# A hybrid DeltaNet and HGRN2 block on one core: gate weights loaded a block ahead, sums of x a pair ahead, and part of a branch's products moved into the first gate's pass

## The chip, the cores and the metric

The kernel runs on one core of a Trainium2 chip. A core has TensorE (PE, the matrix engine), VectorE (DVE), ScalarE (ACT), GpSimd (POOL) and SyncE (SP); here every transfer between DRAM and the on-chip memory is issued from SP's one queue, which is worked off in order. The metric is the device time of one execution in microseconds. Three runs of the kernel before gave 1931.05 us as their median (1929.38 to 1932.9).

## The reference

One layer over 2048 tokens of width 1024, with 16 meta tokens in front. One projection of the normalized input feeds two branches and two gates; the branches are projected back, gated, added and projected out:

```python
proj = rmsnorm(h, norm_w) @ w_in
a_q, a_k, a_v, a_beta, a_alpha, a_z, b_q, b_f, b_i, b_g, gate_a, gate_b = split(proj)
y_a = rmsnorm(gated_deltanet(conv(a_q, a_k, a_v), a_beta, a_alpha), gnorm_a) * silu(a_z)
y_b = rmsnorm(hgrn2(b_q, b_f, b_i), gnorm_b) * silu(b_g)
mixed = sigmoid(gate_a) * (y_a @ w_branch_a) + sigmoid(gate_b) * (y_b @ w_branch_b)
out = rmsnorm(h + mixed @ w_out, final_norm_w)[:, N_META:]
```

The two gates are products of 2048 x 1024 by 1024 x 1024 each, and so is the last projection; w_branch_a and w_branch_b are 512 x 1024.

## The kernel before

**Numbers.** Everything is float32. A large matmul is done with each operand split into two float16 parts (high, and the residual low), as three products of parts. To prepare a weight means: load it raw, take statistics (ACT squares with a sum, or DVE a largest value), find one power of two as its scale, multiply by it (DVE, L212 and L214), round to the high part (ACT, L215), and subtract that for the residual (L216, on DVE or GpSimd). `prepare` is a generator, and one step of it is a block of the statistics or one of eight k-blocks of the split.

**Work units.** Tokens go in 17 chunks of 128 (chunk 0 holds the meta tokens) and, where two go together, in eight pairs. Five stages follow one another:

1. To about 576 us: norm of x, pair by pair (stored as `xs_d`), the projections of the HGRN2 branch b and its chunked scan. `levels` (L684) alternates DVE products QK (L682) with PE matmuls `pl` (L705, L710). As a background, each chunk also runs 2 steps of a weight preparation for branch a's k and v, and 3 steps of the gate weights.
2. 576 to 720 us: the transition, with convolutions of branch a's first pairs and its q and z weights.
3. 720 to about 1290 us: the DeltaNet branch a (convolutions, an inverse by recursion, the scan `scan2`); beside its last pair the first gate's products of pairs 0 and 1.
4. To about 1440 us: the first gate's pass, pairs 2 to 7, with 9 background steps a pair that prepare w_branch_a, w_branch_b and the two halves of w_out.
5. To the end: for each pair the second gate's products, then `merge` for each of its chunks: branch a (24 matmuls `pbr` on w_bra and two additions to the first gate's value), branch b (24 on w_brb), the mix, its split and transposes (`mT`), the 48 matmuls of the last projection (`pout`), the final norm and the store.

**The gates by seven products.** A gate's product for a pair is done as a Strassen-Winograd scheme: a 2 x 2 block product with seven products P1 to P7 for eight, done in the order P1, P2, P6, P7, P5, P3, P4, each of 12 matmuls (`gate_pair`, L446): 84 matmuls a pair. P1, P2 and P4 take x itself, the other four take `xs`, four sums of blocks of x. `left` (L410) makes the sums: seven additions and subtractions on DVE (L428 to L436), three on GpSimd (L439 to L441), and for each sum its high half on ACT (L422) and its low half on DVE (L423); they are kept in `ss_d` for the second gate. `add` (L466) adds each product to its outputs on DVE, and `end` (L469) takes the tanh; the first gate's values go to `ga_d`.

**The gate weights.** `gate_steps` (L343) loads a gate's raw weight in four blocks twice: once for the statistics (even blocks by ACT, L367, odd ones by DVE, L360), once for the seven factors (L377 scales, L381 rounds, L383 and L385 subtract, L392 to L399 form differences). Raw blocks go through one buffer, `gx`; finished factors through three buffers `go` to DRAM (`wg_d`). `gate_part` (L403) reads them back two products at a time, 2 MB. The second gate's first part is requested ahead of the first gate's pass, its other three behind it.

**What sets the order.** Instructions are put in a list per engine by a scheduler that simulates a timeline; `tc.high_priority` draws an instruction ahead, and `tc.issue_after` holds one back. The order on each engine is then fixed, and each engine waits in order. A buffer of a pool is written again only when its last reader is done.

Of the kernel before, what the change touches and what calls it, by code (L numbers as in the profile page):

```python
# [34 lines left out]
POOLC = (3,)  # L35
LAST = (8, 12)
# [23 lines left out]
def hybrid_kernel(ctx: ExitStack, tc: tile.TileContext, x, meta_tokens, norm_w, w_in, conv_w, a_log,  # L60
# [17 lines left out]
    gx = ctx.enter_context(tc.tile_pool(name="gx", bufs=1))  # L78
# [124 lines left out]
    def split_steps(begun, dve=(), scale=None):  # L203
# [16 lines left out]
    def prepare(begun, dst, dve=((), ())):  # L220

        wsl[dst] = yield from split_steps((yield from stats_steps(begun, dve[0])), dve[1],
                                             V)
# [119 lines left out]
    def gate_steps(i, off, pool):  # L343
# [3 lines left out]
        src = w_in[0][:, off:off + D].rearrange("(a k p) (b n) -> p k a b n", a=2, p=P, b=2)  # L347
        stats = tp.tile([P, 16], F32, tag="stats16", name="stats16", bufs=1)
        rows = nw.rearrange("p (a k) -> p a k", a=2)

        def load(k):
            t = gx.tile([P, 2, 2, 512], F32, tag="t8", name="graw")
            for a in range(2):
                SY.dma_start(t[:, a], src[:, k, a])
            return t
        for k in range(4):
            t = load(k)
            st = stats[:, 4 * k:4 * k + 4]
            if k % 2:
                V.tensor_reduce(st, t.rearrange("p a b n -> p (a b) n"), AX.X, ALU.max, apply_absolute_value=True)  # L360
                for a in range(2):
                    V.tensor_scalar(st[:, 2 * a:2 * a + 2], st[:, 2 * a:2 * a + 2], rows[:, a, k:k + 1], None, ALU.mult)
                V.tensor_tensor(st, st, st, ALU.mult)
            else:
                for j in range(4):
                    junk = sp.tile([P, 512], F16, tag="junk", name="junk", bufs=1)
                    A.activation(junk, t[:, j // 2, j % 2], AF.Square, scale=rows[:, j // 2, k:k + 1],  # L367
                                 accum_out=st[:, j:j + 1])
            yield
        sc = scale_of(stats, 16, f"g{i}", GEXP)  # L370
        V.tensor_scalar(hu[:, i:i + 1], sc[:, 1:2], 0.5, None, ALU.mult)
        fac = tp.tile([P, 2, 4], F32, tag="gfac", name="gfac", bufs=1)
        V.tensor_scalar(fac, rows, sc[:, 0:1], None, ALU.mult)
        for k in range(4):
            t = load(k)
            for a in range(2):
                A.activation(t[:, a], t[:, a], AF.Copy, scale=fac[:, a, k:k + 1])  # L377

            def put(n, b, f):
                o = pool.tile([P, 2, 512], F16, tag="go", name="go", bufs=3)  # L380
                A.activation(o[:, 0], b, AF.Copy, scale=f)  # L381
                if f == 1.0:
                    V.tensor_tensor(o[:, 1], b, o[:, 0], ALU.subtract)  # L383
                else:
                    V.scalar_tensor_tensor(o[:, 1], b, f, o[:, 0], ALU.mult, ALU.subtract)  # L385
                SY.dma_start(wg_d[i][:, ORDER.index(n), k], o)
            b11, b12, b21, b22 = t[:, 0, 0], t[:, 0, 1], t[:, 1, 0], t[:, 1, 1]
            put("P1", b11, 1.0)
# [965 lines left out]
```

## Time and profile before

| what | value |
|---|---|
| median of three runs | 1931.05 us (1929.38 to 1932.9) |
| the profiled execution | 1930.47 us, its span 1928.7 us |
| mean granted clock of PE | 0.95 |
| busy in the span: PE, DVE, ACT, POOL | 1747.4, 1360.7, 932.3, 305.2 us |
| instructions | 42,889 |
| moved by DMA | 184.73 MB, mean 96 GB/s |

A busy time is the sum of an engine's instructions, a share is of the span. The granted clock is PE's, as a part of the full speed of 2.4 GHz; a mean below 1 is a mixture with the lower level of 1.2 GHz, at which a matmul of the same shape takes longer. A gap in a row is the idle time of that engine just before the instruction, with the instruction that ended it. The rows themselves stand in a section of their own below.

### The profile page before, as it was taken

How to read it: one execution, taken by the hardware profiler on the slowest of the kernel's cores; microseconds unless marked ns; L12 is line 12 of the kernel's file. 1: busy time of each engine (PE TensorE's matmuls, PEld its weight loads, DVE VectorE, ACT ScalarE, POOL GpSimd, SP SyncE). 2: the span in 40 equal slices, each digit the busy share in tenths (PEclk: the TensorE clock that was granted, in tenths of full speed). 3: DMA queues.
4: the chain of work that ended last, by engine and by line, in shares of the span. 5: the costliest groups of instructions: out<-in, count | busy, mean ns of one | idle time of the engine just before them, and what ended most of it. 6: DMA issues, size and time to landing. Idle time of an engine off the chain costs nothing. (4 is left out here: it accounts for less than half of the span.)

```text
span 1928.7 us, 42889 instructions
## 1 busy us (share of the span) xinstructions
PE 1747.4 (91%) x16763; PEld 1178.6 (61%) x16763; DVE 1360.7 (71%) x5340; ACT 932.3 (48%) x2264; POOL 305.2 (16%) x425
## 2 busy tenths in 40 slices
PE   4599898969999689999999999987789999999997
PEld 3476675746767678888888886553334444444444
DVE  7944776767867978898888799787653444544555
ACT  7655775666756644666656555744321111111211
POOL 3200011101211521222213113233110000000000
PEclk9699899979998889999999999988889999999999
DMA  9013323234250010100100032634373322332121
GB/s 351 33 57 104 123 92 127 100 110 149 78 176 30 12 51 23 40 13 7 34 30 7 13 116 78 229 128 168 143 293 126 121 79 97 101 123 80 58 82 50
DMA packets 56399, 184.73 MB, mean 96 GB/s; under 512 B 6460, under 2 KB 6644, under 8 KB 49028
## 3 DMA queue, kind: packets, MB, share of 16 engines
q1 hardware_dynamic: 56196, 182.00, 26.7%
q8 instruction: 131, 2.15, 0.5%
q14 instruction: 72, 0.59, 0.1%
HBM read 125.35 MB, written 56.62 MB: 94 GB/s over the span
## 5 line engine op out<-in xcount | busy, mean ns | idle before, releaser
L459 PE MATMUL pgate<-wg,xs 128*128 128x512 f16 x768 | 186.3, 397 | 32.5 <-ACT xs L422 29.7
L259 PEld LDWEIGHTS <-x 128*128 128x128 f16 x1368 | 131.7, 99 | 94.9 <-issue 3.3
L1279 PE MATMUL pout<-w_o,mt 128*128 128x512 f16 (+1 forms) x792 | 170.9, 373 | 1.7 <-ACT mt L1267 0.9
L459 PEld LDWEIGHTS <-xs 128*128 128x128 f16 x768 | 77.0, 102 | 127.5 <-ACT xs L422 31.7
L318 DVE SCALAR_TENSOR_TENSOR pair<-raw,cw,pair 128x256 f32<-128x256 f32 (+1 forms) x297 | 138.2, 496 | 6.1 <-ACT pair L312 5.7
L459 PE MATMUL pgate<-wg,x 128*128 128x512 f16 x576 | 132.5, 382 | 4.4 <-ACT gt L472 2.9
L1279 PEld LDWEIGHTS <-mt 128*128 128x128 f16 x792 | 76.8, 98 | 89.5 <-DVE mt L1269 2.3
L939 PEld LDWEIGHTS <-y 128*128 128x128 f16 x768 | 74.6, 98 | 87.1
L459 PEld LDWEIGHTS <-x 128*128 128x128 f16 x576 | 56.6, 99 | 71.4 <-issue 6.7
L1281 DVE SCALAR_TENSOR_TENSOR hres<-pout,mm,hres 128x512 f32<-128x512 f32 (+1 forms) x33 | 24.2, 735 | 102.4 <-PE pout L1279 102.4
L259 PE MATMUL pi<-w_bi,x 128*128 128x512 f16 x408 | 93.9, 384 | 0.0
L267 PE MATMUL pq<-x,w_bq 128*128 128x256 f16 x768 | 93.0, 283 | 0.0
L259 PE MATMUL pg<-w_bg,x 128*128 128x512 f16 x384 | 89.3, 382 | 0.0
L939 PE MATMUL pbr<-w_bra,y 128*128 128x512 f16 x384 | 88.6, 379 | 0.0
L939 PE MATMUL pbr<-w_brb,y 128*128 128x512 f16 x384 | 88.1, 379 | 0.0
L267 PEld LDWEIGHTS <-w_ak 128*128 128x128 f16 x864 | 77.6, 99 | 14.2 <-issue 2.4
L267 PEld LDWEIGHTS <-w_aq 128*128 128x128 f16 x864 | 76.6, 99 | 15.7 <-POOL w_aq L216 3.3
L267 PEld LDWEIGHTS <-w_bq 128*128 128x128 f16 x768 | 77.8, 102 | 11.1
L267 PEld LDWEIGHTS <-w_av 128*128 128x128 f16 x864 | 76.1, 99 | 11.0 <-issue 0.7
L267 PE MATMUL pq<-x,w_bf 128*128 128x256 f16 x672 | 80.1, 277 | 0.0
L1032 DVE TENSOR_TENSOR R<-R,U 128x2 f32<-128x2 f32 (+14 forms) x510 | 78.3, 186 | 0.2
L682 DVE TENSOR_TENSOR QK<-QK,Tb 128x1024 f32<-128x1024 f32 x48 | 61.4, 1279 | 23.4 <-PE pl L710 23.4
(475 smaller groups left out, 4010.4 us busy)
## 6 DMA issues: line engine op xcount, KB each, us to landing
x<-xs_d SPq DMA_DIRECT2D x22, 1024.0 KB, 5.9
graw<-in_w_in_dram SPq DMA_DIRECT2D x32, 512.0 KB, 5.0
wg_d<-go SPq DMA_DIRECT2D x56, 256.0 KB, 2.2
wg<-wg_d SPq DMA_DIRECT2D x6, 2048.0 KB, 7.8
hx<-in_x_dram SPq DMA_DIRECT2D x16, 512.0 KB, 4.1
xs_d<-x SPq DMA_DIRECT2D x8, 1024.0 KB, 4.1
ss_d<-xs SPq DMA_DIRECT2D x8, 1024.0 KB, 3.9
ga_d<-gt SPq DMA_DIRECT2D x16, 512.0 KB, 5.9
```

What stands on the lines that cost most here:

```text
L259: T.matmul(po[:, j:j + cols], xt[:, k, xa, c0:c0 + P], wt[:, k, wa, j:j + cols], start=(n == 0), stop=(n == 23))
L267: T.matmul(po, wt[:, k, wa, h * P:(h + 1) * P], xt[:, k, xa, c0:c0 + ncol], start=(n == 0), stop=(n == 23))
L318: V.scalar_tensor_tensor(av, rows(h, j), wv(j), av, ALU.mult, ALU.add)
L459: T.matmul(po, L[n](k, xa), w[ORDER.index(n)][:, k, wa], start=m == 0, stop=m == 11)
L682: V.tensor_tensor(qk, qk, dv, ALU.mult)
L939: T.matmul(pb, y[:, h, xa, :], w[0][:, 4 * i + h, wa, :], start=(n == 0), stop=(n == 11))
L1032: V.tensor_tensor(R[:, e, c:], R[:, e, c:], U[:, e, c:c + 1].broadcast_to([P, n // 2, 16 - c]), ALU.mult)
L1279: T.matmul(po, mt[:, xa, k, :], wo[i][0][:, k, wa, js], start=(n == 0), stop=(n == 23))
L1281: V.scalar_tensor_tensor(h[:, i, js], po, mm[:, 2 + i:3 + i], h[:, i, js], ALU.mult, ALU.add)
```

## The change

- Gate weights. One generator serves both gates. Raw blocks go in turn into the two halves of `gstage`, a slot of the pool for large weights, and the block after next is requested as soon as one has been read; `go` has seven buffers for three; the pool `gx` goes, and the second gate's last part gets a pool `g8`. Each chunk runs 4 steps for 3. v's weights of branch a are requested behind pair 5, in `gstage`'s slot, and are prepared with 4 steps a chunk from pair 6 on.
- Sums of x. `left` for the next pair is issued ahead of the products of this one, in both gates, and its three GpSimd operations go to DVE.
- Weights of the first gate's pass. The multiplication by the scale is done by ACT, all eight residual subtractions by DVE (before, half by GpSimd). 14 steps run behind pair 2, then 8 behind each.
- Branch a. For chunks 7 to 16 its 24 matmuls a chunk and two additions are done in the first gate's pass (`first_branch`, behind the gate of the next pair); the gate's values wait for them in four buffers `tbs`, and their sum goes to `ga_d`. `merge` does branch a for chunks 1 to 6 only.
- All four parts of the second gate's weights are requested behind the first gate's pass.

The diff, cut to its core:

```diff
@@ split_steps and prepare
         w, raw, rows, tag, stats = begun
         with tc.high_priority(offset=OFS):
             sc = scale_of(stats, KT, tag)
+        if scale is A and rows is not None:
+            fac = tp.tile([P, KT], F32, tag="fac", name="fac")
+            V.tensor_scalar(fac, rows, sc[:, 0:1], None, ALU.mult)
         for k in range(KT):
             t = sp.tile([P, 512], F32, tag="st", name="wsc")
-            if rows is not None:
+            if scale is A:
+                A.activation(t, raw[:, k, :], AF.Copy, scale=sc[:, 0:1] if rows is None else fac[:, k:k + 1])
+            elif rows is not None:
                 E.tensor_scalar(t, raw[:, k, :], rows[:, k:k + 1], sc[:, 0:1], ALU.mult, ALU.mult)
             else:
...
+    def gate_steps(offs, stage, pool):
+        raws = stage.rearrange("p k a n -> p (k a n)").bitcast(F32).rearrange("p (s a b n) -> p s a b n", s=2, a=2, b=2)
+        todo = [(i, k) for i in range(2) for _ in range(2) for k in range(4)]
+        at = [0]
+
+        def load():
+            if at[0] < len(todo):
+                i, k = todo[at[0]]
+                src = w_in[0][:, offs[i]:offs[i] + D].rearrange("(a k p) (b n) -> p k a b n", a=2, p=P, b=2)
                 for a in range(2):
+                    SY.dma_start(raws[:, at[0] % 2, a], src[:, k, a])
+            at[0] += 1
+        load()
+        load()
+        yield
+        for i in range(2):
+            for k in range(4):
+                t = raws[:, k % 2]
...
+                load()
+                yield
...
+            for k in range(4):
+                yield from factor_steps(i, k, raws[:, k % 2], fac, pool)
+                load()
...
-                o = pool.tile([P, 2, 512], F16, tag="go", name="go", bufs=3)
+            o = pool.tile([P, 2, 512], F16, tag="go", name="go", bufs=7)
@@ left
-        G.tensor_tensor(u, a(0, 0, 0), a(1, 0, 0), ALU.subtract)
-        G.tensor_tensor(t, a(0, 0, 1), a(1, 0, 1), ALU.subtract)
-        G.tensor_tensor(u, u, t, ALU.add)
+        V.tensor_tensor(u, a(0, 0, 0), a(1, 0, 0), ALU.subtract)
+        V.tensor_tensor(t, a(0, 0, 1), a(1, 0, 1), ALU.subtract)
+        V.tensor_tensor(u, u, t, ALU.add)
@@ first_gate
         add(prod("P4"), (c21, c21))
         end(c21)
-    def first_gate(q):
+    def first_gate(q, xS, ring=None):
+        if ring is not None:
+            gate_pair(0, xS, wga, [ring[:, (2 * q + j) % 4] for j in range(2)])
+            return
         t = [raw_t("gt0").rearrange("p h i -> p (h i)")[:, :D], acc_t("gt1")]
         t = [x.rearrange("p (a n) -> p a n", a=2) for x in t]
-        gate_pair(0, left(q, True), wga, t)
+        gate_pair(0, xS, wga, t)
         for j in range(2):
             SY.dma_start(ga_d[2 * q + 1 + j], t[j])
@@ the loop over pairs of the first stage
                         qx = query(xnext)
                 if p > 0:
                     with tc.issue_after(mark["A"].ins), tc.issue_after(mark["V"].ins):
-                        run_steps(bg, LAST[i] if last else 2)
+                        run_steps(bg, LAST[i] if last else 2 if p < NP_ - 2 else 4)
                         if not last:
-                            run_steps(gsteps, 3)
+                            run_steps(gsteps, 4)
             if p == 0:
-                gsteps = chain(gate_steps(0, OFF_GA, p1), gate_steps(1, OFF_GB, p1))
+                stage = wp.tile([P, KT, 2, 512], F16, tag="w", name="gstage")
+                gsteps = gate_steps((OFF_GA, OFF_GB), stage, p1)
+                run_steps(gsteps, 1)
                 beg["k"] = in_begin(OFF_K, "ak")
+                bg = prepare(beg["k"], "k")
+            if p == NP_ - 3:
+                run_steps(gsteps)
                 beg["v"] = in_begin(OFF_V, "av")
-                bg = chain(prepare(beg["k"], "k"), prepare(beg["v"], "v"))
+                bg = chain(bg, prepare(beg["v"], "v"))
         scan1(*prev)
@@ the first gate's pass
+        def first_branch(q):
+            for j in range(2):
+                t = tbs[:, (2 * q + j) % 4]
+                branch(2 * q + 1 + j, ya_d, wsl["bra"], t)
+                SY.dma_start(ga_d[2 * q + 1 + j], t)
         fnw = p1.tile([P, D], F32, name="fnw")
         SY.dma_start(fnw, final_norm_w.rearrange("(o d) -> o d", o=1).broadcast_to([P, D]))
         beg["bra"] = br_begin(w_branch_a, gna, "bra")
         beg["brb"] = br_begin(w_branch_b, gnb, "brb")
         beg["o0"], beg["o1"] = out_begin(0, wx), out_begin(1, wx)
-        wgb = gate_part(1, 0, wp)
-        bg = chain(prepare(beg["bra"], "bra", ((), EVEN)), prepare(beg["brb"], "brb", ((), EVEN)),
-                   prepare(beg["o0"], "o0", (HALF, EVEN)), prepare(beg["o1"], "o1", (HALF, EVEN)))
-        for q in range(2, NP_):
-            first_gate(q)
-            run_steps(bg, 9)
-        run_steps(bg)
-        wgb += [f for j in (1, 2, 3) for f in gate_part(1, j, wp if j < 3 else gx)]
         tbs = wp.tile([P, KT, 2, 512], F16, tag="w", name="tbs")
         tbs = tbs.rearrange("p k a n -> p (k a n)").bitcast(F32).rearrange("p (c a n) -> p c a n", c=4, a=2)
+        ALL = tuple(range(KT))
+        bg = chain(prepare(beg["bra"], "bra", ((), ALL), A), prepare(beg["brb"], "brb", ((), ALL), A),
+                   prepare(beg["o0"], "o0", (HALF, ALL), A), prepare(beg["o1"], "o1", (HALF, ALL), A))
+        xS = left(2, True)
+        for q in range(2, NP_):
+            xn = left(q + 1, True) if q + 1 < NP_ else left(0, False)
+            first_gate(q, xS, tbs if q >= LAG else None)
+            xS = xn
+            run_steps(bg, 14 if q == 2 else 8)
+            if q > LAG:
+                first_branch(q - 1)
+        run_steps(bg)
+        first_branch(NP_ - 1)
+        wgb = [f for j in range(4) for f in gate_part(1, j, wp if j < 3 else g8)]
         wba, wbb, wo = wsl["bra"], wsl["brb"], [wsl["o0"], wsl["o1"]]
         us = p1.tile([P, 4], F32, name="us")
@@ the last stage
-        def second_gate(q):
-            gate_pair(1, left(q, False), wgb, [tbs[:, (2 * q + j) % 4] for j in range(2)])
+        def second_gate(q, xS):
+            gate_pair(1, xS, wgb, [tbs[:, (2 * q + j) % 4] for j in range(2)])
         def merge(c, tb):
             mix = raw_t("mix").rearrange("p h i -> p (h i)")[:, :D].rearrange("p (a n) -> p a n", a=2)
             SY.dma_start(mix, ga_d[c])
-            branch(c, ya_d, wba, mix)
+            if c <= 2 * LAG:
+                branch(c, ya_d, wba, mix)
             h = acc_t("hres").rearrange("p (a n) -> p a n", a=2)
             SY.dma_start(h, xf[(c - 1) * P:c * P, :].rearrange("t (a n) -> t a n", a=2))
             V.scalar_tensor_tensor(hf, hf, r, fnw, ALU.mult, ALU.mult)
             SY.dma_start(of[(c - 1) * P:c * P, :], hf)
-        second_gate(0)
+        second_gate(0, xS)
         for q in range(NP_):
             if q + 1 < NP_:
-                second_gate(q + 1)
+                second_gate(q + 1, left(q + 1, False))
             for j in range(2):
                 merge(2 * q + 1 + j, tbs[:, (2 * q + j) % 4])
```

Where the instructions now stand, at three places. First, DVE at the sums of x for pair 6. Before, they stand behind the scaling of w_out (`wsc<-w_o`) and an addition of pair 5 (`gt`); `s` is the sum, `s1l` its low parts:

```order
L216 TENSOR_TENSOR w_o_18834<-wsc,w_o_18834 128x512
L214 TENSOR_SCALAR wsc<-w_o_18834,sc_o_19503 128x512
L466 TENSOR_TENSOR gt_19543<-gt_19544,pgate 128x512
L214 TENSOR_SCALAR wsc<-w_o_18834,sc_o_19503 128x512
L428 TENSOR_TENSOR s_19548<-x 128x512
L216 TENSOR_TENSOR w_o_18834<-wsc,w_o_18834 128x512
L429 TENSOR_TENSOR s1l<-x 128x512
L430 TENSOR_TENSOR s_19548<-s_19548,s1l 128x512
L423 SCALAR_TENSOR_TENSOR xs<-s_19548,xs 128x4x128
```

After, for the same pair:

```order
L447 TENSOR_TENSOR s_19457<-s_19457,s1l 128x512
L456 TENSOR_TENSOR s_19472<-x 128x512
L457 TENSOR_TENSOR s3l<-x 128x512
L483 TENSOR_TENSOR tbs<-tbs,pgate 128x512
L440 SCALAR_TENSOR_TENSOR xs<-s_19457,xs 128x4x128
L458 TENSOR_TENSOR s_19472<-s_19472,s3l 128x512
L450 TENSOR_TENSOR s_19457<-s_19457,x 128x512
L966 SCALAR_TENSOR_TENSOR tbs<-tbs,pbr 128x512
L483 TENSOR_TENSOR tbs<-tbs,pgate 128x512
L450 TENSOR_TENSOR s_19457<-s_19457,x 128x512
L440 SCALAR_TENSOR_TENSOR xs<-s_19472,xs 128x4x128
```

The scalings are gone from between them; the additions that stand among them (`tbs<-tbs,pgate`) are those of pair 5, whose products run meanwhile, and one of branch a (`pbr`).

Second, PE at pair 7, from its second product (P2, on x) to the next. Before, P6 on the sums follows at once:

```order
L459 MATMUL pgate<-wg_17638,x 128x512
L459 LDWEIGHTS x
L459 MATMUL pgate<-wg_17638,x 128x512
L459 LDWEIGHTS xs
L459 MATMUL pgate<-wg_17640,xs 128x512
L459 LDWEIGHTS xs
```

After, 13 matmuls of branch a stand in between:

```order
L476 MATMUL pgate<-wg_17623,x 128x512
L476 LDWEIGHTS x
L476 MATMUL pgate<-wg_17623,x 128x512
L964 LDWEIGHTS y
L964 MATMUL pbr<-w_bra,y 128x512
L964 LDWEIGHTS y
L964 MATMUL pbr<-w_bra,y 128x512
```

A wait for the sums of pair 7 would now be met behind these 13 matmuls.

Third, DVE in the first stage at the statistics of the first gate's weights. Before, one reduction of a raw block stands there (the other one is 85 rows behind):

```order
L682 TENSOR_TENSOR QK<-QK,ff 128x2x512
L560 TENSOR_SCALAR Lg<-sg 128x512
L360 TENSOR_REDUCE stats_2452<-graw 128x4
L714 COPY_PREDICATED PD<-k_175,pl 128x64x2
L682 TENSOR_TENSOR QK<-QK,Tb 128x2x256x2
L556 TENSOR_REDUCE ba<-pba 128x8
L631 SCALAR_TENSOR_TENSOR Lg<-sg,Lg 128x512
L362 TENSOR_SCALAR stats_2452<-stats_2452,nw 128x2 x2
L363 TENSOR_TENSOR stats_2452<-stats_2452 128x4
```

After, both odd blocks' reductions stand close together:

```order
L617 SCALAR_TENSOR_TENSOR L<-qx,L 128x512
L372 TENSOR_REDUCE stats_2451<-gstage 128x4
L619 TENSOR_TENSOR qx<-qx,L 128x512
L374 TENSOR_SCALAR stats_2451<-stats_2451,nw 128x2 x2
L708 TENSOR_TENSOR QK<-qx,ff 128x1024
L375 TENSOR_TENSOR stats_2451<-stats_2451 128x4
L372 TENSOR_REDUCE stats_2451<-gstage 128x4
L715 COPY_PREDICATED PD<-k_172,pl 128x256
L702 TENSOR_TENSOR QK<-QK,ff 128x2x512
```

Between the two reductions stand four rows, and the second one reads the half of `gstage` that the first has just freed.

## Rows read from the trace of the kernel before

**Rows 1.** The page's busy time by engine (share of the span, instructions)
```profile
PE 1747.4 (91%) x16763; PEld 1178.6 (61%) x16763; DVE 1360.7 (71%) x5340; ACT 932.3 (48%) x2264; POOL 305.2 (16%) x425
```

**Rows 2.** Busy time by stage: span, PE, PEld, DVE, ACT, POOL, clock, DMA, GB/s
```profile
192.00:576.00 384.00, 336.93 (x4497) 247.32 (x4498) 275.92 (x724) 252.78 (x495) 52.33 (x38) 0.93 0.35 120
576.00:720.00 144.00, 117.53 (x1471) 97.46 (x1469) 115.96 (x415) 87.19 (x245) 48.26 (x61) 0.85 0.09 31
...
1248.00:1440.00 192.00, 153.65 (x819) 74.50 (x818) 139.21 (x372) 77.93 (x162) 50.85 (x40) 0.88 0.49 181
1440.00:1928.70 488.70, 478.23 (x2425) 226.10 (x2423) 236.99 (x486) 83.26 (x135) 0.00 (x0) 0.99 0.28 95
```

**Rows 3.** Timeline of PE, first gate's pass: start, duration, instructions, gap before
```profile
1293.34 5.66 PE L459 MATMUL pgate<-wg,xs 128*128 128x512 f16 x14 [2.19 <-ACT xs L422]
...
1326.01 6.85 PE L459 MATMUL pgate<-wg,xs 128*128 128x512 f16 x24 [6.62 <-ACT xs L422]
...
1353.45 10.52 PE L459 MATMUL pgate<-wg,xs 128*128 128x512 f16 x48
...
1384.87 13.31 PE L459 MATMUL pgate<-wg,xs 128*128 128x512 f16 x48 [12.19 <-ACT xs L422]
...
1415.56 8.14 PE L459 MATMUL pgate<-wg,xs 128*128 128x512 f16 x24 [8.68 <-ACT xs L422]
```

**Rows 4.** Groups by form, 1290 to 1440: busy, mean ns of one, gaps before
```profile
L459 PE MATMUL pgate<-wg,xs 128*128 128x512 f16 x240 | 65.2, 438 | 31.1 <-ACT xs L422 29.7 <-DVE gt L466 1.5
...
L466 DVE TENSOR_TENSOR gt<-gt,pgate 128x512 f32<-128x512 f32 x34 | 22.8, 684 | 39.0 <-PE pgate L459 38.9
L423 DVE SCALAR_TENSOR_TENSOR xs<-s,xs 128x512 f16<-128x512 f32 x19 | 15.6, 834 | 4.2 <-ACT xs L422 3.9
...
L439 POOL TENSOR_TENSOR s<-x 128x512 f32<-128x512 f16 x4 | 6.0, 1500 | 1.5 <-issue 1.3
...
L436 DVE TENSOR_TENSOR s<-s,x 128x512 f32<-128x512 f32 x5 | 3.4, 685 | 0.1
```

**Rows 5.** Timeline of DVE at the sums for pair 6
```profile
1374.88 0.78 DVE L214 TENSOR_SCALAR wsc<-w_o,sc_o 128x512 f32<-128x512 f32 x1
1375.58 0.68 DVE L428 TENSOR_TENSOR s<-x 128x512 f32<-128x512 f16 x1
...
1376.90 1.52 DVE L429 TENSOR_TENSOR s1l<-x 128x512 f32<-128x512 f16 x1
```

**Rows 6.** Timeline of DVE at the second gate's statistics, and its wait, 190 to 576
```profile
387.88 2.29 DVE L360 TENSOR_REDUCE stats<-graw 128x4 f32<-128x2048 f32 x1 [4.33 <-DMA graw<-in_w_in_dram]
...
404.49 2.29 DVE L360 TENSOR_REDUCE stats<-graw 128x4 f32<-128x2048 f32 x1 [2.29 <-DMA graw<-in_w_in_dram]
...
DVE stats L360 <- DMA graw<-in_w_in_dram: 6.6, 2, 4.3
```

**Rows 7.** Timeline of PE at the same place
```profile
391.98 1.06 PE L705 MATMUL pl<-QK 128*32 128x16 f32 x64 [6.72 <-DVE QK L682]
...
410.13 0.61 PE L166 MATMUL np<-stats,k 128*128 128x16 f32 x2 [4.26 <-DVE stats L363]
```

**Rows 8.** Waits of ACT, 190 to 660: total, times, longest
```profile
ACT go L381 <- DMA wg_d<-go: 14.3, 8, 2.7
ACT graw L377 <- DMA graw<-in_w_in_dram: 12.6, 5, 3.5
```

**Rows 9.** Busy time in two stretches of 48 us, columns as in rows 2
```profile
384.00:432.00 48.00, 32.25 (x357) 23.09 (x355) 28.43 (x96) 30.63 (x69) 3.77 (x3) 0.79 0.33 111
...
1152.00:1200.00 48.00, 45.91 (x437) 33.24 (x438) 45.33 (x277) 28.05 (x95) 15.00 (x28) 1.00 0.24 93
```

**Rows 10.** The page's DMA issues: count, KB each, us from issue to landing
```profile
x<-xs_d SPq DMA_DIRECT2D x22, 1024.0 KB, 5.9
graw<-in_w_in_dram SPq DMA_DIRECT2D x32, 512.0 KB, 5.0
...
wg<-wg_d SPq DMA_DIRECT2D x6, 2048.0 KB, 7.8
```

**Rows 11.** Timeline of PE at the second last chunk's end
```profile
1896.79 0.60 PE L1279 MATMUL pout<-w_o,mt 128*128 128x512 f16 x2 [0.73 <-ACT mt L1267]
1897.87 10.10 PE L1279 MATMUL pout<-w_o,mt 128*128 128x512 f16 x46 [0.48 <-DVE mt L1269]
```

More of the change, by code (lines that the diff above doesn't have):

```diff
@@ L35 @@
 POOLC = (3,)
+LAG = 3
 LAST = (8, 12)
@@ L77, in hybrid_kernel @@
     ap = ctx.enter_context(tc.tile_pool(name="ap", bufs=1))
-    gx = ctx.enter_context(tc.tile_pool(name="gx", bufs=1))
     PSUM = {}
@@ L218, in split_steps, with prepare @@
         return w, sc[:, 1:2], sc[:, 0:1]
-    def prepare(begun, dst, dve=((), ())):
-        wsl[dst] = yield from split_steps((yield from stats_steps(begun, dve[0])), dve[1],
-                                             V)
+    def prepare(begun, dst, dve=((), ()), scale=None):
+        wsl[dst] = yield from split_steps((yield from stats_steps(begun, dve[0])), dve[1], scale)
     def run_steps(steps, n=None):
@@ new lines, in gate_steps @@
+        load()
+        load()
+        yield
+        for i in range(2):
+            stats = tp.tile([P, 16], F32, tag="stats16", name="stats16", bufs=1)
+            for k in range(4):
+                t = raws[:, k % 2]
+                st = stats[:, 4 * k:4 * k + 4]
+                if k % 2:
+                    V.tensor_reduce(st, t.rearrange("p a b n -> p (a b) n"), AX.X, ALU.max, apply_absolute_value=True)
+                    for a in range(2):
+                        V.tensor_scalar(st[:, 2 * a:2 * a + 2], st[:, 2 * a:2 * a + 2], rows[:, a, k:k + 1], None, ALU.mult)
+                    V.tensor_tensor(st, st, st, ALU.mult)
+                else:
+                    for j in range(4):
+                        junk = sp.tile([P, 512], F16, tag="junk", name="junk", bufs=1)
+                        A.activation(junk, t[:, j // 2, j % 2], AF.Square, scale=rows[:, j // 2, k:k + 1],
+                                     accum_out=st[:, j:j + 1])
+                load()
+                yield
+            sc = scale_of(stats, 16, f"g{i}", GEXP)
+            V.tensor_scalar(hu[:, i:i + 1], sc[:, 1:2], 0.5, None, ALU.mult)
+            fac = tp.tile([P, 2, 4], F32, tag="gfac", name="gfac", bufs=1)
+            V.tensor_scalar(fac, rows, sc[:, 0:1], None, ALU.mult)
+            for k in range(4):
+                yield from factor_steps(i, k, raws[:, k % 2], fac, pool)
+                load()
@@ new lines, in factor_steps, with put @@
+    def factor_steps(i, k, t, fac, pool):
+        for a in range(2):
+            A.activation(t[:, a], t[:, a], AF.Copy, scale=fac[:, a, k:k + 1])
+        def put(n, b, f):
+            o = pool.tile([P, 2, 512], F16, tag="go", name="go", bufs=7)
+            A.activation(o[:, 0], b, AF.Copy, scale=f)
+            if f == 1.0:
+                V.tensor_tensor(o[:, 1], b, o[:, 0], ALU.subtract)
+            else:
+                V.scalar_tensor_tensor(o[:, 1], b, f, o[:, 0], ALU.mult, ALU.subtract)
+            SY.dma_start(wg_d[i][:, ORDER.index(n), k], o)
+        b11, b12, b21, b22 = t[:, 0, 0], t[:, 0, 1], t[:, 1, 0], t[:, 1, 1]
+        put("P1", b11, 1.0)
+        put("P2", b21, 1.0)
+        put("P3", b22, 2.0)
+        yield
+        V.tensor_tensor(b11, b12, b11, ALU.subtract)
+        put("P5", b11, 2.0)
+        V.tensor_tensor(b12, b22, b12, ALU.subtract)
+        put("P7", b12, 2.0)
+        yield
+        V.tensor_tensor(b22, b22, b11, ALU.subtract)
+        put("P6", b22, 2.0)
+        V.tensor_tensor(b21, b21, b22, ALU.subtract)
+        put("P4", b21, 1.0)
+        yield
@@ L858, in hybrid_kernel @@
                     run_steps(bg)
-                    run_steps(gsteps)
                     xt = xpair(0)
@@ L928, in hybrid_kernel @@
     mp = cg.enter_context(tc.tile_pool(name="mp", bufs=1))
+    g8 = cg.enter_context(tc.tile_pool(name="g8", bufs=1))
     def branch(c, y_d, w, t):
@@ L1202, in hybrid_kernel @@
                         if p == NP_ - 2:
-                            wga = [f for j in range(4) for f in gate_part(0, j, wp if j < 3 else gx)]
+                            wga = [f for j in range(4) for f in gate_part(0, j, wp if j < 3 else g8)]
                 else:
-                    first_gate(i)
+                    first_gate(i, left(i, True))
             xt = xn
```

50 lines of the change are left out of this document (removed).

## The prediction

> **What bounds the kernel now.** I read the share of busy time first [rows 1]: TensorE (PE) works 1747.4 of 1928.7 us, so no more than 181 us of the span are without a matmul, and only where they lie can a reordering win anything. The table by stages [rows 2] says where. In the last stage (from 1440 us) PE is busy for 478 of 489 us at full clock: there is nothing to win there. The two stages to look at are the long first one (192 to 576 us: 47 us without a matmul, granted clock 0.93) and the first gate's pass (1248 to 1440 us: 38 us without a matmul, a mean granted clock of 0.88, that is part of the time at the lower of its two levels, 1.2 instead of 2.4 GHz). The transition between (576 to 720 us) lacks 26 us, but the change barely touches it.
>
> In the first gate's pass the timeline of PE [rows 3] names one waiter: the products on xs, the sums of x. Four waits, 2.19, 6.62, 12.19 and 8.68 us (pairs 3, 4, 6, 7), 29.7 us together, all before the first xs product of a pair, and none for pair 5 (third row), whose sums were early. Other bubbles of the pass (38.35 − 29.7) come to about 8 us. After a long wait the same matmuls run slower: 48 take 10.52 us behind no wait (0.219 us each) and 13.31 us behind the wait of 12.19. Over the window 1290 to 1440 the 240 xs matmuls take 65.2 us [rows 4], against 240 × 0.219 = 52.6 us: 12.6 us are the price of the lower clock level.
>
> Why the sums are late stands in the order of VectorE (DVE), not in the transfer: DVE scales w_o, then begins pair 6's first sum at 1375.58, and its next additions take 1.52 us each [rows 5], where the same form alone takes 0.685 us [rows 4]. The GpSimd sums of the same pair (1.50 us each, rows 4) run beside them.
>
> In the first stage DVE stops at 387.88 for 4.33 us and at 404.49 for 2.29 us, for raw gate weights [rows 6]; PE is out for 6.72 us before 391.98 and 4.26 us before 410.13 [rows 7]. ACT waits 14.3 us for output buffers of the gate weights to be written away and 12.6 us for raw blocks [rows 8]. Around 400 us the clock is 0.79 [rows 9].
>
> **The change, part by part.** All sums are made against the profiled execution, 1930.47 us with a span of 1928.7; the median of the runs is 1931.05, 0.6 us higher.
>
> *The first gate's pass.* In the new order the sums of a pair stand among the additions of the pair before, and 48 matmuls of the first branch stand with each pair from 4 on. PE then has per pair 84 × 0.219 = 18.4 us of gate and 48 × 0.219 = 10.5 us of branch, 28.9 us. DVE has in the same time 10 sums at 0.685 (three of them from GpSimd), 4 splits at 0.83, 7 gate additions and 4 branch additions at 0.684, and at most 8 residuals of weights at about 0.685: 6.9 + 3.3 + 4.8 + 2.7 + 5.5 = 23.2 us. So DVE keeps ahead of PE from pair 4 on, and the scalings of weights, which stood before the sums, have gone to ACT, which is busy for 78 of 192 us there [rows 2]. A load of x lands 5.9 us after its issue [rows 10]; it can start when the pair two before has freed its buffer, so 5.9 us and about 10 us of sums fit into 28.9. Hence the waits of pairs 4, 6 and 7 (27.5 us) go, pair 3's 2.19 us shrinks at best (no branch work yet in its time: 18.4 us of PE against some 20 of DVE). I take 27 of 29.7 us. Of the 12.6 us of slow clock I take 9, since the tail of branch a's scan still makes bubbles of 1 to 2 us near pairs 3 and 4; of the other 8 us, 1. That is −37 us. Bounds: −15 if the fillers and sums only halve the waits and the clock stays; −50 if all waits, all clock and the other bubbles go.
>
> The branch work itself is the same 384 + 384 matmuls, moved by 10 chunks of 24, 53 us, from the last stage, where PE was full: zero in itself. Its transfers go along: per chunk a load of y and a store of the result, both on SP's one queue, which also carries the loads of x. The stores wait for DVE, and the load of the pair after next stands behind two of them. These stores belong to a branch that is done a pair earlier, so I cost this at 0; if it is not, the third rival below has the price.
>
> *A rule that speaks for more.* After each long wait the rows show dearer matmuls. The Trainium skill, "TensorE: Matmul & The Clock Gate", section "HAM oscillation — how this bites in real kernels", says that an idle gap is paid a second time, in a lower clock behind it; by it the whole 12.6 us would come back and the term would be −41 instead of −37. The rows agree in the direction.
>
> *Gate weights in the first stage.* The same 32 steps are done, four a chunk instead of three. With seven output buffers for three the 14.3 us of ACT go; with the raw block requested two blocks ahead most of the 12.6 us go. What PE sees of it: 6.72 and 4.26 us behind statistics, and of ACT's 26.9 us behind factor steps perhaps a quarter, so some 18 us in all, and a little clock. But the statistics are not cured. There are two half-slots, and in the new order the two reductions of a gate stand five rows of DVE apart (below 3 us of work at these row times), while the block between them is asked for only when the first has been read, and takes 5.0 us to land [rows 10]: DVE still waits about 2 to 3 us, now for the first gate too, which had no such wait (only two of DVE's statistics waited in the first stage, rows 6). I take −6: about 10 won in the factor steps, 4 lost or kept in the statistics. Bounds −20 (all waits and the clock of rows 9) and +10 (four new waits of 2.5 us, nothing won).
>
> *v's weights* start about two pairs later; their last 4 steps fall beside the last pair and the convolutions of the transition, where DVE is busy for 116 of 144 us. Four steps are four scalings and residuals; at 0.685 us each that is 4 × 1.37 = 5.5 us, and up to 4 × 2.2 = 9 us where one of the two takes the 1.5 of rows 5; I take about half as hidden beside PE's work: +3 (0 to +8; not below nothing, since the work is the same and only comes where DVE is busier).
>
> *DVE's three more sums* for pairs 0 and 1 fall at 1104 to 1200 us, where DVE is busy for 45.3 of 48 us [rows 9]: 2 × 3 × 0.685 = 4.1 us, most of it where PE has scan work queued: +1 (0 to +4). Here the Trainium skill, "Perfetto Trace Analysis", section "Optimizing Scalar/DVE Operations", speaks against the change: where DVE is saturated, handing work to ScalarE or even GpSimd may pay. By it the term would be the whole +4.1. It adds that the two share a port, and the 1.52 us of rows 5 beside GpSimd agree, so I stay with +1.
>
> *The end.* At the last chunk boundaries PE waits 0.73 + 0.48 us for the transposed mix [rows 11]; with branch a's matmuls gone three such boundaries lack a filler instead of two. +2 (0 to +4).
>
> *Second gate's weights* are all requested after the first pass now; one of four parts was early before. 2 MB land in 7.8 us [rows 10]. Its buffer comes free after the second product of pair 7, with 60 gate matmuls (13 us) and the last branch behind it: 0, hidden by these; 7.8 us if that cover is gone.
>
> Sum: −37 − 6 + 3 + 1 + 2 = −37 us; 1930.5 − 37 = 1893.5, said 1894.
>
> **Rivals.**
> 1. *Only the first pass works, and by half* (waits move to the queue or to pairs 3 and 4, no gain in the first stage): −15 + 6 = −9 to −20, so 1910 to 1922. For it: SP's queue is in order, and the last chunk of the scan still sits in pairs 3 and 4. Against it: 23.2 us of DVE against 28.9 of PE. Chance 0.17.
> 2. *Both stages work fully*: −50 − 20 + 6, about 1867. For it: the chain of cause is the same in rows 3 and 7. Against: the statistics' waits. Chance 0.10.
> 3. *Slower.* One mechanism, on SP: loads of x and of the second gate's weights stand behind stores of branch results that wait for PE. If these stores end late, each pair from 4 to 7 waits for the 5.9 us of its x plus 10 us of sums after it: 16 us each, and the fillers cannot cover it, since they are what the queue waits for. Three such pairs cost 48 us against the 42 (29.7 + 12.6) that are lost now, and 7.8 us come for the weights: +14, about 1944 (1934 if the first stage wins 10, 1960 with a fourth pair). It decides from the point where a store is done later than the end of its pair's last gate product. Chance 0.09.
> 4. *The reordering does nothing*, because the waits that go are replaced one for one: 1930 ± 4. Chance 0.04.
>
> **How the numbers follow.** My forecast (−25 to −50 us) has 0.60, 1894 us, its own range 1881 to 1906. Rival 1 has 0.17, rival 2 0.10, rival 3 0.09, rival 4 0.04. The range for 8 in 10 leaves out most of rivals 3 and 4 and the ends of 1 and 2: 1866 to 1920. 0.2% of the time is 3.9 us, what can be told from no change. Faster 0.87, same 0.04, slower 0.09.
>
> **What would show it.** In the profile after: no wait of PE over 3 us for xs from pair 4 on, 48 xs matmuls of a pair in 10.5 us, the granted clock of the first pass at 0.95 or more; GpSimd with only the scan's last splits there; the stage from the first gate's pass to the end 35 us shorter together. In the first stage: no wait of ACT for stores of gate weights, and PE stops behind a statistics reduction that are shorter, not gone. I am wrong if PE waits for x instead of xs, if SP holds loads of x behind stores of the branch, or if the first stage becomes longer.

## The result, and the profile after

| | before | after |
|---|---|---|
| median of four runs | 1931.97 us (1929.38 to 1933.32) | 1868.49 us (1864.67 to 1870.26) |
| span of the profiled execution | 1928.7 us | 1868.5 us |
| mean granted clock | 0.95 | 0.966 |

The ratio is 0.967 (95% interval 0.9651 to 0.969): 63 us less, where 37 were forecast. The direction held. The time did not keep to the forecast's own range, 1881 to 1906 us: it lies beside the 1867 us of rival 2 (both stages work fully), which had a chance of 0.10. The term of the first gate's pass came out about as forecast; the term of the gate weights was far too small.

The page's busy time by engine, which answers to [rows 1]:

```profile
PE 1734.6 (93%) x16763; PEld 1171.8 (63%) x16763; DVE 1333.9 (71%) x5350; ACT 949.3 (51%) x2296; POOL 251.0 (13%) x385
```

The same number of matmuls takes 12.8 us less of PE's time, at a mean granted clock of 0.966 for 0.95, and the span loses 60.2. To see where, both traces are cut at events that both have: an update of branch b's state by PE (`pu`) near 193 us and the one five pairs later, the first product of branch a's scan (`pks`), the first product of a gate (`pgate`), the end. Before (columns as in rows 2):

```profile
192.50:555.50 363.00, 316.43 (x4314) 231.95 (x4315) 264.34 (x684) 238.03 (x463) 49.91 (x36) 0.92 0.35 120
555.50:762.96 207.46, 180.48 (x2173) 148.43 (x2171) 167.41 (x773) 119.56 (x330) 59.13 (x85) 0.89 0.11 38
762.96:1176.02 413.06, 409.40 (x4563) 352.31 (x4561) 360.78 (x2388) 247.58 (x806) 92.30 (x200) 1.00 0.10 36
1176.02:1928.70 752.68, 697.35 (x3792) 339.99 (x3789) 438.87 (x1169) 205.91 (x424) 68.65 (x69) 0.96 0.35 122
```

After:

```profile
193.20:527.40 334.20, 308.84 (x4313) 226.78 (x4314) 251.54 (x666) 233.71 (x457) 42.66 (x30) 0.96 0.37 128
527.40:739.60 212.20, 181.20 (x2175) 147.42 (x2173) 175.77 (x787) 122.63 (x336) 67.22 (x91) 0.90 0.12 42
739.60:1152.66 413.06, 409.38 (x4562) 352.37 (x4560) 360.66 (x2390) 247.61 (x806) 90.36 (x198) 1.00 0.10 36
1152.66:1868.50 715.84, 688.68 (x3792) 338.24 (x3789) 415.92 (x1177) 224.63 (x456) 15.52 (x30) 0.98 0.36 128
```

Row by row: −28.8, +4.7, 0.0 and −36.8 us (the first mark itself comes 0.7 us later). The first stage's row holds the surprise: PE idles 25.4 us there (334.20 − 308.84) where it idled 46.6, and does the same matmuls in 7.6 us less. What went are waits of PE for VectorE, 37.2 us in the first row before and 15.2 after, most of them of the matmuls `pl` for a QK product. The largest, before and after (total, times, longest; `ba` is a small reduction right behind a QK product):

```profile
PE pl L705 <- DVE QK L682: 11.3, 4, 6.7
PE pl L710 <- DVE QK L682: 10.8, 6, 4.3
```
```profile
PE pl L730 <- DVE ba L576: 7.0, 2, 4.4
PE pl L730 <- DVE QK L702: 4.7, 3, 2.5
```

In the first gate's pass the waits of [rows 3] are gone. The page's groups of the products, for the whole program, before and then after:

```profile
L459 PE MATMUL pgate<-wg,xs 128*128 128x512 f16 x768 | 186.3, 397 | 32.5 <-ACT xs L422 29.7
...
L459 PE MATMUL pgate<-wg,x 128*128 128x512 f16 x576 | 132.5, 382 | 4.4 <-ACT gt L472 2.9
```
```profile
L476 PE MATMUL pgate<-wg,xs 128*128 128x512 f16 x768 | 175.1, 379 | 2.5 <-DVE gt L483 2.5
...
L476 PE MATMUL pgate<-wg,x 128*128 128x512 f16 x576 | 136.4, 388 | 2.0 <-DVE gt L483 2.0
```

30 us of waits and 11.2 us of slow matmuls went with xs. The products on x became 3.9 us dearer, 2.4 of them behind a new wait, in PE's timeline of the changed kernel:

```profile
1332.32 0.60 PE L166 MATMUL np<-stats,k 128*128 128x8 f32 x2 [7.53 <-ACT junk L199]
1332.77 7.77 PE L476 MATMUL pgate<-wg,x 128*128 128x512 f16 x24
1340.37 5.34 PE L476 MATMUL pgate<-wg,xs 128*128 128x512 f16 x24
```

PE stands 7.53 us at the small product that makes w_out's scale, since ACT still takes the statistics of a w_out that was requested only at 1321.4; the next 24 matmuls take 7.77 us for 5.34. (Another 2.0 us lie near 1197, behind four gaps of 0.4 to 1.4 us in branch a's last scan: 12 products on x take 4.75 us there for 2.75.)

In the first stage the waits of DVE for ACT at the gate weights' factors fell, and those for the statistics did not (6.6 us in both, for before in [rows 6]). Before and after, 190 to 560 us:

```profile
DVE go L383 <- ACT go L381: 21.3, 8, 5.6
...
DVE go L385 <- ACT go L381: 4.9, 5, 1.6
```
```profile
DVE stats L372 <- DMA gstage<-in_w_in_dram: 6.6, 2, 4.1
DVE go L400 <- ACT go L398: 5.0, 2, 3.7
DVE go L402 <- ACT go L398: 0.3, 1, 0.3
```

Both waits for statistics are the second gate's, as before. PE feels less of them: the 4.26 us of [rows 7] are gone, and in place of the 6.72 it stands 2.50 us behind the second one:

```profile
323.76 2.29 DVE L372 TENSOR_REDUCE stats<-gstage 128x4 f32<-128x2048 f32 x1 [2.50 <-DMA gstage<-in_w_in_dram]
...
327.86 1.07 PE L730 MATMUL pl<-QK 128*32 128x32 f32 x32 [2.50 <-DVE QK L702]
```

### The profile page after: what moved, and what is told of

Its sections match the earlier page's. It is cut to its first block, busy times and chain, and to the rows that moved or that the text cites. A ratio compares the mean times of both kernels' runs of the same rounds, so it can differ in the third digit from the quotient of the medians.

```text
span 1868.5 us, 42842 instructions
## 1 busy us (share of the span) xinstructions
PE 1734.6 (93%) x16763; PEld 1171.8 (63%) x16763; DVE 1333.9 (71%) x5350; ACT 949.3 (51%) x2296; POOL 251.0 (13%) x385
## 5 line engine op out<-in xcount | busy, mean ns | idle before, releaser
L476 PE MATMUL pgate<-wg,xs 128*128 128x512 f16 x768 | 175.1, 379 | 2.5 <-DVE gt L483 2.5
L476 PE MATMUL pgate<-wg,x 128*128 128x512 f16 x576 | 136.4, 388 | 2.0 <-DVE gt L483 2.0
L483 DVE TENSOR_TENSOR tbs<-tbs,pgate 128x512 f32<-128x512 f32 x91 | 61.2, 684 | 69.6 <-PE pgate L476 67.8
L1319 ACT ACTIVATE mix<-hres 128x512 f32<-128x512 f32 x32 | 20.1, 629 | 162.8 <-DVE hres L1318 131.9
L486 ACT ACTIVATE tbs<-tbs,hu 128x512 f32<-128x512 f32 x52 | 37.4, 720 | 124.0 <-DVE tbs L483 123.8
```

Source lines behind the costliest of these rows:

```text
L476: T.matmul(po, L[n](k, xa), w[ORDER.index(n)][:, k, wa], start=m == 0, stop=m == 11)
L483: V.tensor_tensor(d, s, po, ALU.add)
L486: A.activation(d, d, AF.Tanh, scale=hu[:, i:i + 1])
L1319: A.activation(mix[:, i], h[:, i], AF.Square, scale=D ** -0.5, accum_out=ss[:, i:i + 1])
```

## The experiments

Two theories stood after the result. Theory 1: the first stage's gain is waiting that went (output buffers, raw blocks). Theory 2: it is where the steps lie (four a chunk, pairs 5 and 6 without gate work). The ratios are to the kernel before, run on the same chip. What a run lost is its median less the changed kernel's 1868.49 us, which was not run again beside it; before's median beside the experiments was 1930.6 to 1933.3 us.

**e1, the gate-weight part alone; e2, the other part alone.** e1 is the changed kernel with the loops over `first_gate` and `merge`, `left` and `prepare` as before; e2 the changed kernel with `gate_steps`, `gx`, v's weights and the number of steps as before. One edit of each:

```diff
@@ e1
-            xn = left(q + 1, True) if q + 1 < NP_ else left(0, False)
-            first_gate(q, xS, tbs if q >= LAG else None)
+            first_gate(q, left(q, True))
@@ e2
-                            run_steps(gsteps, 4)
+                            run_steps(gsteps, 3)
```

> The gate-weight part alone (stage, seven buffers, four steps a chunk, v's weights late); the first gate's pass, the sums of x and branch a as before. The landmarks of the two traces (first gate product at 1176.0 before, 1152.7 after) say 23 us: 1909 us, if the parts simply add. My own sum before the result gave this part -6 + 3 = -3: 1929 us. Rival: the 23 us need the other part too (order of the scheduler shifts everything): then between 1915 and 1930.

> The other part alone: sums a pair ahead and on VectorE, scaling on ScalarE, ten chunks of branch a in the first pass; the gate weights as before. By the landmarks (first gate product to the end: 752.7 us before, 715.8 after) 37 us: 1895 us if the parts add. Rival (interaction): over 1900.

Measured: e1 1905.35 us (0.9875, interval 0.9849 to 0.99), e2 1891.6 us (0.9803, 0.977 to 0.9835), before 1931.67. 26.3 and 40.1 us make 66.4, the whole change 63: the parts add, and the gate weights' part is worth some 25 us, not 3.

**e3, blocks requested where they are used.**

```diff
-        load()
-        load()
...
+                load()
                 t = raws[:, k % 2]
```

> The changed kernel, but each raw block of the gate weights is requested where it is used instead of two blocks ahead; still two halves, seven output buffers and four steps a chunk. Theory 1 (the waits for raw blocks cost PE most of their length): most of the 23 us are lost, about 1885 us. Theory 2 (the gain comes from where the steps lie: four a chunk, so that pairs 5 and 6 have none): 1868 to 1874 us.

Measured: 1869.82 us (0.9684, 0.9652 to 0.9715), the changed kernel's time. It does not speak for theory 2, since the edit did not do what it was for: ACT's waits for raw blocks stayed as they were, 6.4 us and 6.7, in e3 and then in the changed kernel:

```profile
ACT gstage L392 <- DMA gstage<-in_w_in_dram: 6.4, 3, 2.7
```
```profile
ACT gstage L394 <- DMA gstage<-in_w_in_dram: 6.7, 3, 2.9
```

In e3's trace the requests of the second gate's blocks leave within 1.1 us of the changed kernel's: the scheduler requests a block as soon as its half is free, wherever the line stands. What is ahead is set by the number of halves.

**e4, three steps a chunk.**

```diff
-                            run_steps(gsteps, 4)
+                            run_steps(gsteps, 3)
```

> The changed kernel with three gate steps a chunk instead of four, blocks still requested ahead: the steps reach to the end of pair 5, with a few run at once there. Theory 1 (waits): still 1868 to 1874 us. Theory 2 (where the steps lie): pair 5 has gate work again, about 8 us are lost, 1876 us or more.

Measured: 1879.47 us (0.9742, 0.9716 to 0.9767), 11 us lost, as theory 2 has it, but only in part where it has it. The first product of branch a's scan comes at 741.73 us (739.60 in the changed kernel), 2 us later, and 25 matmuls that stand ahead of it in the changed kernel (`pc`, a convolution for k) stand behind it in e4. In the changed kernel these 25 take:

```profile
736.25 2.90 PE L271 MATMUL pc<-xm,w_ak 128*128 128x256 f16 x25
```

So the same work of the first stages is done some 5 us later. The stage behind it is longer, too:

```profile
741.73:1162.41 420.68, 414.22 (x4601) 355.18 (x4598) 368.58 (x2402) 249.22 (x813) 91.16 (x198) 1.00 0.10 36
```

It takes 420.7 us for 413.1. Of these 7.6 us, 4.8 are matmuls (414.22 for 409.38), since the 25 and 13 others from behind the stage now fall into it; 2.8 are idle time. The edit does not touch this stage, but the scheduler put another order there: PE's matmuls between the two marks stand in the same order in before, the changed kernel, e1, e2, e3, e7 to e10 and e12 (413.0 to 413.1 us), and differ in e4, e5, e6 and e11 (418.5 to 420.7 us). So theory 2 has a part, but not the whole: the place of the steps is worth some 2 to 5 us of the first stages, an estimate from one profile. VectorE waits no longer for ACT at the factors than in the changed kernel (4.2 us for 5.3), so this part is not that wait.

**e5, three output buffers; e6, one half for all raw blocks.**

```diff
@@ e5
-            o = pool.tile([P, 2, 512], F16, tag="go", name="go", bufs=7)
+            o = pool.tile([P, 2, 512], F16, tag="go", name="go", bufs=3)
@@ e6
-                    SY.dma_start(raws[:, at[0] % 2, a], src[:, k, a])
+                    SY.dma_start(raws[:, 0, a], src[:, k, a])
...
```

> The changed kernel with three output buffers for the gate weights' factors instead of seven. Theory A (ScalarE's waits for the buffers' writes, 14.3 us before, hold VectorE and through it the QK products that PE waits for): the waits return, 10 to 20 us lost, 1880 to 1888 us. Theory B (the raw blocks' second half is what counts): under 4 us lost.

> The changed kernel with all raw blocks of the gate weights in one half of the stage, each requested where it is used, as the single buffer before: what is requested ahead is gone for good, since the half must be free first. Theory A (output buffers): under 5 us lost, below 1874 us. Theory B (raw blocks): 10 to 20 us lost, 1880 to 1888 us.

Measured: e5 1884.89 us (0.9759, 0.9722 to 0.9796), e6 1888.59 us (0.9775, 0.9741 to 0.9808). Both waits came back, in e5 for the buffers, in e6 for the blocks:

```profile
ACT go L398 <- DMA wg_d<-go: 12.6, 10, 2.6
DVE go L400 <- ACT go L398: 10.0, 5, 3.8
```
```profile
ACT gstage L392 <- DMA gstage<-in_w_in_dram: 19.0, 9, 3.7
DVE go L398 <- ACT go L396: 12.7, 8, 3.2
```

VectorE's waits for ACT at the factors are 14.6 us in e5 (10.0 and another 4.6) and 12.7 in e6, for the changed kernel's 5.3. The rows from the `pu` near 193 us to the one five pairs later, e5 and then e6:

```profile
191.60:529.40 337.80, 305.12 (x4313) 225.23 (x4314) 253.00 (x666) 233.82 (x457) 42.29 (x30) 0.96 0.37 126
```
```profile
194.10:534.10 340.00, 307.02 (x4287) 225.69 (x4287) 255.02 (x663) 233.49 (x455) 40.07 (x30) 0.95 0.37 125
```

PE idles 32.7 and 33.0 us in them, where it idles 25.4 in the changed kernel and 25 to 29 in the seven other runs that have its order on PE up to the scan. So with each wait some 4 to 8 us of idle time of PE came back, and both fit theory 1; before had 46.6.

In the whole time the parts are harder to tell. 5.4 us of each loss lie in branch a's stage in its other order (418.5 for 413.1), though 20 of its matmuls stand ahead of its first mark there. Up to that mark, the scan's first product, the profiles lose 3.0 us in e5 (742.63) and 10.8 in e6 (750.35); some 2.4 us of each are these 20 matmuls, done early. With everything old, e2's mark lies at 755.57, 16 us behind the changed kernel's, and before's at 762.96, although both have one order on PE up to there; the eight kernels with the changed kernel's order have it at 735.4 to 740.6. Single profiles of one order thus differ by 5 to 7 us at this mark. The second half may be worth more than the buffers, but that is not shown, and the losses of e4, e5 and e6 up to the mark together (some 14 us, the moved matmuls counted) do not make up the 16 to 23, as far as single profiles can tell. One more difference was not parted: the changed kernel's order of PE's matmuls in the first stage is not before's, and an order alone cost time in branch a's stage.

**e7, no branch work in the pass; e8, sums not ahead.**

```diff
@@ e7
-LAG = 3
+LAG = 8
-        first_branch(NP_ - 1)
@@ e8
-            xn = left(q + 1, True) if q + 1 < NP_ else left(0, False)
-            first_gate(q, xS, tbs if q >= LAG else None)
+            first_gate(q, left(q, True), tbs if q >= LAG else None)
```

> The changed kernel with branch a's products of chunks 7 to 16 back in the last stage; sums of x still a pair ahead, no GpSimd. By my sum 18.4 us of PE a pair stand against 20.5 us of VectorE without the branch's additions: waits for xs of about 2 us a pair from pair 3 on return, and some slow clock: 1878 to 1888 us. Rival (the sums ahead were enough): 1868 to 1874 us.

> The changed kernel with the sums of x issued in front of their own pair's products instead of a pair ahead; branch a's products still moved as fillers. If being issued ahead is what removes the waits: each of pairs 4 to 7 waits for up to 7 us, 1885 to 1895 us. Rival (the fillers and the freed VectorE do it, since the scheduler draws the sums ahead by itself): 1868 to 1874 us.

Measured: e7 1879.15 us (0.9729, 0.9696 to 0.9763), e8 1877.3 us (0.9714, 0.9671 to 0.9757): about 10 and 9 us of some 40. Neither is the cause alone. The waits of PE, 1150 to 1480 us, in e7 and in e8:

```profile
PE np L166 <- ACT junk L199: 10.2, 1, 10.2
PE pgate L476 <- DVE gt L483: 8.1, 6, 1.9
PE yT L792 <- ACT yp L787: 6.8, 1, 6.8
```
```profile
PE pbr L964 <- DMA y<-ya_d: 4.6, 2, 3.0
PE pgate L476 <- ACT xs L439: 4.4, 1, 4.4
PE pgate L476 <- DVE gt L483: 3.1, 4, 1.8
```

In e7 no wait for xs came back, against my sum; what fillers hid is the end of branch a's scan (`yT`, 6.8 us), and PE waits longer for w_out's scale (10.2 us for 7.5) and for the gate's additions (8.1 for 4.6). In e8 one wait for xs is back, 4.4 us, not four of 7, and loads of y cost 4.6 us: it seems that, as with the loads in e3, the scheduler draws sums ahead by itself when VectorE has room.

**e9, the old share of engines; e12, only the sums back on GpSimd.**

```diff
@@ e9 and e12
-        V.tensor_tensor(u, a(0, 0, 0), a(1, 0, 0), ALU.subtract)
+        G.tensor_tensor(u, a(0, 0, 0), a(1, 0, 0), ALU.subtract)
...
@@ e9
-        bg = chain(prepare(beg["bra"], "bra", ((), ALL), A), prepare(beg["brb"], "brb", ((), ALL), A),
+        bg = chain(prepare(beg["bra"], "bra", ((), EVEN)), prepare(beg["brb"], "brb", ((), EVEN)),
```

> The changed kernel with the old share of engines in the first gate's pass: three sums a pair and half of the residuals on GpSimd, the scaling of the weights on VectorE. Sums a pair ahead and fillers stay. Theory 1 (GpSimd makes VectorE's additions twice as dear, 1.52 us for 0.68, so that sums and weights come late): 1878 to 1888 us. Theory 2 (with 28.9 us of PE a pair there is room for it): 1868 to 1874 us.

> The changed kernel with only the three sums a pair back on GpSimd; weights are scaled on ScalarE and their residuals made on VectorE as in the changed kernel. It parts the 20 us that the old share of engines cost. If the sums on GpSimd (beside which VectorE's additions take 1.5 us) are the cause: 1880 us or more. If the scaling on VectorE and the residuals on GpSimd are: 1868 to 1874 us.

Measured: e9 1889.01 us (0.9778, 0.976 to 0.9796), 20 us lost; e12 1869.64 us (0.9689, 0.9657 to 0.9721), nothing lost. So the sums alone may be on GpSimd; the share of the weights' preparation, alone or together with the sums, is what counts. In e12 VectorE's additions beside GpSimd did become dearer, 1187 ns for the 698 of the changed kernel, and it cost no time (groups of 1150 to 1420 us, changed kernel and e12):

```profile
L446 DVE TENSOR_TENSOR s1l<-x 128x512 f32<-128x512 f16 x7 | 4.9, 698 | 0.0
```
```profile
L446 DVE TENSOR_TENSOR s1l<-x 128x512 f32<-128x512 f16 x7 | 8.3, 1187 | 0.0
```

In e9 the weights' scalings on VectorE (32 of 0.64 to 0.70 us) come on top, and GpSimd's residuals take 1.25 to 1.44 us each; PE waits 10.2 us for w_out's scale, 7.2 us for the gate's additions and 6.8 us for the scan's end. The first of these is as long in e12 (10.3 us), which lost nothing; the other two are e9's own (2.0 and 0.5 us in e12). Which of the two moves (scaling or residuals) costs more was not parted.

**e10, w_out's steps later; e11, v's weights a pair earlier as well.**

```diff
@@ e10 and e11
-            run_steps(bg, 14 if q == 2 else 8)
+            run_steps(bg, (14, 5, 5, 8, 8, 8)[q - 2])
@@ e11
-            if p == NP_ - 3:
+            if p == NP_ - 4:
-                        run_steps(bg, LAST[i] if last else 2 if p < NP_ - 2 else 4)
+                        run_steps(bg, LAST[i] if last else 2 if p < NP_ - 3 else 3)
```

> The changed kernel with other numbers of background steps behind pairs 2 to 7: 14, 5, 5, 8, 8, 8 for 14, 8, 8, 8, 8, 8, so that w_out's statistics stand later. The largest wait that is left in the changed kernel's first pass (7.5 us of PE on the scale of w_out, whose load stands on SP behind loads of y) should go, with some slow clock: 1858 to 1863 us. Rival (the wait only moves to the next product that needs a late weight): 1867 to 1872 us.

> The kernel of e10 with v's weights one pair earlier too: requested behind pair 4, three steps a chunk in pairs 5 and 6, none left for pair 7. The changed kernel gives back 7 us between pair 7 and the first scan (28 us ahead at the last projection of pair 7, 21 to 24 us behind it); if that is v's late steps, up to 7 us less than e10. Rival (the order of the branch a stage, which this edit changes, costs as much): as e10 or up to 8 us more.

Measured: e10 1858.09 us (0.962, 0.9604 to 0.9636), 10 us below the changed kernel and the fastest of all; e11 1865.19 us (0.9659, 0.9645 to 0.9674). In e10 the load of w_out is requested later still (1329.1 us), but the product that needs its scale stands further back in PE's order, and the wait is gone; the stretch that held it, in the changed kernel and in e10:

```profile
1296.00:1344.00 48.00, 40.47 (x196) 19.49 (x195) 27.19 (x63) 24.57 (x57) 1.16 (x1) 0.89 0.55 203
```
```profile
1289.00:1337.00 48.00, 48.00 (x247) 23.40 (x246) 32.82 (x67) 21.11 (x42) 1.16 (x1) 1.00 0.41 151
```

e11 lost 7 us to e10. Its branch a's stage is the one of e4, with 38 matmuls more (420.6 us for 413.1); its scan begins at 738.56, e10's at 737.64, with 25 matmuls still to do, so v's place won nothing.

## Why the prediction was right, and where it was not

- *As a whole*: −63 us lies beyond the forecast's −25 to −50 and at the lower end of the range for 8 in 10 (1866 to 1920). Rival 2 has the time, but not the way to it: it put −50 on the first gate's pass and −20 on the gate weights, and the runs have −36.8 and −28.8.
- *What bounds the kernel* held: both places named are the ones that gave time, and branch a's stage gave none (413.06 us before and after).
- *The first gate's pass*, −37 with +2 for the end: the measured stretch from the first gate product on lost 36.8 us. No wait of PE for xs is left, 24 xs matmuls take 5.34 us, and from 1290 to 1440 us the granted clock is 0.97 and GpSimd is busy for 1.2 us, as said. The sum is right partly by luck, by errors that cancel: the xs waits and their slow clock gave 41 us, more than the 36 taken; smaller waits gave some 5 more (the scan's end `yT` alone 4.6 us before, none after), where 1 was taken; and the new wait for w_out's scale took back 7.5 with 2.4 us of slow matmuls. I had priced only transfers that a step moved on the queue, not the small product of a scale, which waits on PE with the whole gate behind it. Of the 12.6 us of slow clock, of which I took 9, 11.2 came back with the gaps, and the new gap was paid a second time in the 24 matmuls behind it. The Trainium skill, "TensorE: Matmul & The Clock Gate", section "HAM oscillation — how this bites in real kernels", says that work behind such a wait starts at the lower clock; the trace agrees, 7.77 us for 5.34 behind a wait of 7.53.
- *My reason for the late sums* was half right: the order on VectorE fits (no wait is left), though e8, with the sums issued where they were, has only one back; the dearer additions beside GpSimd do not count by themselves (e12), and the weights' scaling and residuals do (e9).
- *Gate weights*, −6 (−20 to +10): this step failed. The stretch lost 28.8 us, outside its bounds. The wrong step is the size of what PE sees: "of ACT's 26.9 us behind factor steps perhaps a quarter", and 4 us "lost or kept in the statistics". VectorE's waits for ACT at the factors fell from 26.2 to 5.3 us, PE's waits for VectorE from 37.2 to 15.2, and PE's idle time by as much, 21.2 us, with 7.6 us less for the same matmuls. Of the 22.0 us, 8.5 are the two stops behind statistics (6.72 and 4.26, now 2.50), where a loss was taken, and 13.5 the rest, half of the 26.9. VectorE's own waits for statistics did stay, two of them, 6.6 us; but the first gate was not without such a wait before, as the prediction had it: it had 2.4 us at 166 us, ahead of where [rows 6] begins (3.3 us after). I had counted the two waits of PE that stood behind a reduction; the QK products stand behind the factors' subtractions on the same VectorE, and PE waits for them. e5 brings the waits for buffers back, and PE's waits for VectorE rise with them to 25.2 us; e6 brings back those for blocks, and they rise to 19.6 us, which is 4.4 of the 7.6 us more that PE idles there. How much each is worth in time, beside the place of the steps (e4), stays open.
- *v's weights*, +3 (0 to +8): +4.7 between the first stage's last mark and the scan, in size. That v's late steps are its cause is not shown: e11 took them away and won nothing.
- *DVE's three sums*, +1: 0.0 in branch a's stage; e12, with the sums back on GpSimd, is neither faster nor slower. The Trainium skill, "Perfetto Trace Analysis", section "Optimizing Scalar/DVE Operations", says that moving work off a saturated VectorE, even to GpSimd, may make sense, but that between these two it might not help, since they share a port; e12 agrees with the second half, 1869.64 us for 1868.49.
- *The second gate's weights*, 0: no wait for them. *Rival 3*'s queue did not strike: SP waits, and VectorE waits 6.9 us for loads of x in the pass, but PE waits for no sum.

## What to carry to other kernels

A wait of one in-order engine for another can count at nearly its full length for a third that hangs on the same engine: here 20.9 us less of VectorE's waits for ACT went with 22.0 us less of PE's waits for VectorE. A trace names only the last link, so add up the waits along the chain and not only the waits that carry the transfer's name. Under a list scheduler, where a request stands in the code can say little (e3): how many buffers there are sets what is ahead. And look whether an edit changed the order of stages that it does not touch: here that went with 5 to 8 us, as much as the effect in question, in four of twelve runs. Then count the matmuls between the marks as well, since work moves across them.

## What the runs showed of the hardware

A store of the gate weights landed 4.2 us after its issue in the changed kernel where it took 2.2 before (median), and nothing waited for it any more: a longer landing cost nothing once a buffer was there to write. The number of buffers alone does not set it: it is 3.0 us in e5 with three, and 2.2 in e6 with seven buffers and one half for the blocks.
